# Attention values as wide products in an encoder block: one product of 256 columns instead of two of 128, with the evacuations, tile rings and load queues that go with it

## The chip, the cores and the metric

The kernel runs on one core of a Trainium2 chip. The metric is the device time of one execution in microseconds (us). The kernel before was run three times; a separate execution was profiled.

## The reference

It is one layer of a hybrid encoder on 1024 tokens of width 1024, all in float32:

```python
h = h + 0.5 * swiglu(rms_norm(h, ffn1_norm[i]), ffn1_w_gate[i], ffn1_w_up[i], ffn1_w_down[i])
u = rms_norm(h, mix_norm[i])
z = u @ w_in[i]
q, k, v, s_in, gates = jnp.split(z, splits, axis=-1)
y_attn = neighbourhood_attention(q, k, v, na_rpb[i]) @ w_attn_out[i]      # 8 heads of 64
y_ssm = s5_branch(s_in, ...) @ w_ssm_out[i]
g_attn, g_ssm = jnp.split(jax.nn.sigmoid(gates), N_BRANCH, axis=-1)
h = h + (g_attn * y_attn + g_ssm * y_ssm) @ w_out[i]
h = h + 0.5 * swiglu(rms_norm(h, ffn2_norm[i]), ffn2_w_gate[i], ffn2_w_up[i], ffn2_w_down[i])
h = h + (p[i] @ ple_w_proj[i]) * jax.nn.sigmoid(rms_norm(h, ple_norm[i]) @ ple_w_gate[i])
...
return rms_norm(h, final_norm)
```

Tokens stand on a grid of 16 rows by 64. In `neighbourhood_attention` a token sees a window of 8 rows by 16 columns that is clamped inside the grid; scores get a learned bias per head and relative place, then softmax, then the weighted sum of the values. `s5_branch` runs a diagonal complex state space layer forward and backward over the tokens, in 32 groups of 16 channels with 64 states each, then a gated linear unit.

## The kernel before

Every float32 product with weights is made of three products of a rounded format (fp32r): an operand is split in a high part, cast by ACT, and the rest, subtracted by DVE (`split`), and `mm3` (L182 to L186) multiplies high by high, high by rest and rest by high into one bank of 128x512. TensorE (PE) runs its instructions in the order of the program. The orders of DVE, ACT, POOL (GpSimd) and SP, which issues most loads, come from a scheduler that plans all engines on a time line of its own.

The order of stages is the first feed-forward block, the mixer, the second feed-forward block, the per-layer input and the last norm (`end`, with the last statistics in `fin[2].stat`). The change lies in the mixer and in `end`.

In the mixer two streams are woven on TensorE. The main one makes the projections of u by `mm3`, of which the gate tiles (`gt`) and the q and k tiles come last. The side stream is a generator, `mixer_side`, which gets a turn every few `mm3`. It works through 64 attention units (8 heads, two halves of the rows `rb`, four blocks of columns `cb`). At step j:

- `attn_scores` of unit j: two products of q with the high and the rest of k into `s` (288 or 384 columns); DVE adds the bias and takes the maximum, ACT makes the softmax `sm`.
- `attn_turn` of unit j-3: three transposes of `sm` into bank `pt`; ACT casts `pth` from it, DVE subtracts `ptl`.
- `attn_values` of unit j-5: for each of three groups of keys one product of `pth` with 128 weight columns (`vhl`: 64 of the high part of v and 64 of the rest) and one of `ptl` with the 64 high columns alone, each over 128 query columns of a bank `O`. One bank takes the four `cb` of a half. After the fourth, ACT copies the lower 64 partitions (`ol`), DVE adds (`ot`), and the queue of ACT stores 64x512 to `o_d` in DRAM.
- `scan_steps(2)`: two steps of the state space scan on POOL, three instructions each (L1092 to L1094), 128 steps in all on the states X.
- from j = 48 on: `ssm_out` of a pair of groups, which issues four loads (`emi`: output matrices from `e_d` and inputs from `u_d`, two each, L1102 and L1103) and copies states to `xs`; three steps later `go` of that pair makes its outputs `yo` with two products L1117 and four L1119, which ACT copies to `ys` and stores.

After that come the gated linear unit, the loads of both branches (`load_br`: `br` from `o_d` for b = 0, from `y2_d` for b = 1, through a ring of three tiles of 128x1024 called "st"), the branch products, and the output projection, whose weights `wblk` POOL loads with an accumulating load (L415).

Tiles come from rings: "hid", 56 tiles of 128x512, of which u takes 32; "w", 12 tiles of 128x1024; "tmp", 4; "st", 3. TensorE writes to 8 banks of 128x512.

Of the kernel before, what the change touches and what calls it, by code (L numbers as in the profile page):

```python
# [8 lines left out]
F32 = mybir.dt.float32  # L9
# [7 lines left out]
P = 128  # L17
SEQ = 1024
HT = 512
# [19 lines left out]
def encoder_block(ctx, tc, I, out):  # L39
# [76 lines left out]
    o_d = dtile("o_d", [512, SEQ])  # L116
    g_d = dtile("g_d", [16, P, SEQ])
    y_d = dtile("y_d", [NPD, P, NCH])
    y2_d = dtile("y2_d", [512, SEQ])
# [81 lines left out]

        return tc.issue_after(mark["ins"]) if "ins" in mark else nullcontext()

    def rstd(m, r, q):
        A.activation(r, m, AF.Abs_reciprocal_sqrt, bias=eps)
        V.tensor_tensor(q, r, r, ALU.mult)
        V.scalar_tensor_tensor(q, m, eps, q, ALU.add, ALU.mult)
        V.scalar_tensor_tensor(r, q, -3.0, r, ALU.add, ALU.mult)

    class Norm:  # L210
# [33 lines left out]
        def stat(self, r=None, summed=False):  # L244
            if summed:
                m = self.acc
            else:
                m = bank("ms")[:, 0:self.n]
                sums = [self.acc] + self.more
                for i, sq in enumerate(sums):  # L250
                    T.matmul(m, lhsT=ones, rhs=sq, start=i == 0, stop=i == len(sums) - 1)
            q = tmq("rq", [P, self.n])
            r = thid("rs", [P, self.n], F32) if r is None else r
            rstd(m, r, q)
            self.r = r

        def apply(self, gi, res, every):
# [839 lines left out]
    def ssm_out(pr):  # L1097

        ms = []
        for g in range(2):  # L1100
            em = thid("emi", [P, 4, NCH], F32)
            nc.sync.dma_start(em[:, 0:3].rearrange("p a b -> p (a b)"), e_d[2 * pr + g])  # L1102
            nc.sync.dma_start(em[:, 3], u_d[2 * pr + g])  # L1103
            ms.append(em)

        xs = tw("xs", [P, 2, 2, NCH], F32)
        for g in range(2):
            for r in range(2):
                s0 = Xv[g * 64:(g + 1) * 64, r, pr, 0:1]
                both = bass.AP(tensor=s0.tensor, offset=s0.offset, ap=[list(s0.ap[0]), [NCH + 2, 2], [1, NCH]])  # L1110
                (A.copy if g == r else V.tensor_copy)(xs[r * 64:(r + 1) * 64, g], both)

        def go():
            o = bank("yo")
            for g in range(2):
                oo = o[:, g * NCH:(g + 1) * NCH]
                T.matmul(oo, lhsT=ms[g][:, 0], rhs=ms[g][:, 3], start=True, stop=False)  # L1117
                for d in range(2):
                    T.matmul(oo, lhsT=ms[g][:, 1 + d], rhs=xs[:, g, d], start=False, stop=(d == 1))  # L1119
            ys = tmp("ys", [P, 2, NCH])  # L1120
            A.copy(ys, o[:, 0:2 * NCH].rearrange("p (g c) -> p g c", g=2))
            nc.scalar.dma_start(y_d[2 * pr:2 * pr + 2].rearrange("g p c -> p g c"), ys)
        return go
# [10 lines left out]
    def qk_proj(hp, wq, wk):  # L1134
        qs, kh, kl = [], [], []
        for t in range(2):
            o = proj(wq, t, "q")
            for i in range(2):
                if t == 0:
                    qs.append(tw("qs"))  # L1140
                src = o[i * 64:(i + 1) * 64].rearrange("p (r b c) -> p r b c", r=8, b=4)
                hs, ls = slice(i * 64, (i + 1) * 64), slice((1 - i) * 64, (2 - i) * 64)

                def view(sl):
                    return qs[i][sl, hsl(t)].rearrange("p (b r c) -> p r b c", b=4, r=8)
                A.copy(view(hs), src)
                V.tensor_tensor(view(ls), src, view(hs).bitcast(F32), ALU.subtract)
        for t in range(2):
            o = proj(wk, t, "k")
            for i in range(2):  # L1150
                if t == 0:
                    kh.append(tw("kh"))
                    kl.append(tw("kl"))
                hs, ls = slice(i * 64, (i + 1) * 64), slice((1 - i) * 64, (2 - i) * 64)
                A.activation(kh[i][hs, hsl(t)], o[hs], AF.Copy, scale=0.125)
                A.activation(kh[i][ls, hsl(t)], o[hs], AF.Copy, scale=0.125)
                for s_ in (hs, ls):
                    V.scalar_tensor_tensor(kl[i][s_, hsl(t)], o[hs], 0.125, kh[i][hs, hsl(t)].bitcast(F32),
                                           ALU.mult, ALU.subtract)
        for i in range(2):  # L1160
            qkv[2 * hp + i] = (qs[i], kh[i], kl[i])

    def load_v(hd, cb):
        n = 4 * KNC[cb]
# [33 lines left out]
    def attn_scores(hd, rb, cb):  # L1198
        q, kh, kl = qkv[hd]
        n = KNC[cb]  # L1200
        nk = 12 * n
        qv = q[:, rb * HT + cb * P:rb * HT + (cb + 1) * P]
# [12 lines left out]
        V.reciprocal(st[:, 2:3], st[:, 1:2])  # L1215
        A.activation(sm, sm, AF.Copy, scale=st[:, 2:3])
        return sm

    def attn_turn(cb, sm):
        kp = 4 * KNC[cb]  # L1220
        tp = bank("pt")
        for g in range(3):
            T.transpose(tp[0:kp, ksl(g)], sm[:, g * kp:(g + 1) * kp], ident)
# [4 lines left out]
        return ph, pl  # L1228

    def attn_values(hd, rb, cb, O, ph, pl):  # L1230
        kp = 4 * KNC[cb]
        hl = vld[hd, cb]
        for g in range(3):

            T.matmul(O[:, ksl(cb)], lhsT=hl[0:kp, rb + g].rearrange("p h d -> p (h d)"), rhs=ph[0:kp, ksl(g)], start=(g == 0), stop=False,
                     skip_group_check=True)
            T.matmul(O[0:64, ksl(cb)], lhsT=hl[0:kp, rb + g, 0], rhs=pl[0:kp, ksl(g)], start=False, stop=(g == 2),
                     skip_group_check=True)
        if cb == 3:
            ot, ol = tmp("ot"), tmp("ol")  # L1240
            A.copy(ol[0:64], O[64:128])
            V.tensor_tensor(ot[0:64].rearrange("p (r b c) -> p b r c", r=8, b=4),
                            O[0:64].rearrange("p (b r c) -> p b r c", b=4, r=8),
                            ol[0:64].rearrange("p (b r c) -> p b r c", b=4, r=8), ALU.add)
            nc.scalar.dma_start(o_d[hd * 64:(hd + 1) * 64, hsl(rb)], ot[0:64])


    ydr = y_d.rearrange("g (t o) c -> g o t c", o=16)
# [37 lines left out]
    def mixer_side():  # L1286
# [31 lines left out]
        for j in range(n + 6):  # L1318
            if j < n:
# [3 lines left out]
                if cb == 0 and j > 0:  # L1323
                    make_tabs(hd, rb)
                sms[j] = attn_scores(hd, rb, cb)
            if 0 <= j - 3 < n:
                pts[j - 3] = attn_turn(units[j - 3][2], sms.pop(j - 3))
            if 0 <= j - 5 < n:
                hd, rb, cb = units[j - 5]
                if cb == 0:  # L1330
                    O[hd, rb] = bank("O")
                attn_values(hd, rb, cb, O[hd, rb], *pts.pop(j - 5))
                if rb == 1 and hd + 1 < NH:
                    load_v(hd + 1, cb)
            scan_steps(2)
            if j >= SO:
                p = j - SO
# [62 lines left out]
    def load_br(t, b):  # L1400

        res = []
        if b == 0:
            for k in range(0, 4, 2):
                st = tst("br")
                nc.sync.dma_start(st.rearrange("p (k c) -> p k c", k=2),
                                  o_d[k * P:(k + 2) * P, hsl(t)].rearrange("(k p) c -> p k c", p=P))
                for i in range(2):
                    hi, lo = tx("bh"), tx("bl")
                    split(hi, lo, st[:, hsl(i)])  # L1410
                    res.append((hi, lo))
            return res
        for k in range(4):
# [264 lines left out]
    def end():  # L1678
# [131 lines left out]
```

## Time and profile before

| | |
|---|---|
| median of three runs | 2099.49 us (2098.23 to 2099.73) |
| profiled execution | 2096.29 us, its span 2094.5 us |
| granted TensorE clock, mean | 0.998 |
| TensorE busy | 2074.5 us, 99% of the span |
| DVE, ACT, POOL busy | 1416.1, 999.6 and 399.4 us |
| last scan step on POOL | starts at 1009.9 us |
| yo products | 1029.0 to 1099.5 us |

Rows of the timeline give start, duration, engine, line, operation, output and inputs, shape; "x3" means three alike in a row, and a bracket at the end the idle time before and what ended it. In a table by stage, the numbers are the length, the busy time of the engines with counts, the clock granted (1.00 is full), the share of the DMA engines that was busy and GB/s. In a tile's rows the three numbers are shortest, median and longest in ns, and then the first and last start in us. Matmuls overlap, so the time of one in a stream is the distance to the next start.

### The profile page before, as it was taken

Reading aid. Unit: us, or ns where it says so; the run is one execution under the profiler, and the core shown is the slowest. Engines: PE = TensorE matmul, PEld = TensorE weight load, DVE = VectorE, ACT = ScalarE, POOL = GpSimd, SP = SyncE. Lnnn points to the kernel's source line nnn. Section 1 sums busy time; section 2 is a strip of 40 time slices with the busy share of each in tenths; the row PEclk is TensorE's granted clock in tenths of the full one; section 3 lists DMA queues with packets and bytes.
Section 4 is the critical chain, followed back from the end, with each engine's and each line's share of the span. In section 5 each row is a group of like instructions: output and inputs, shape, how many; then the busy total and the mean of one; then the engine's idle time right before and its main releaser. Section 6 shows DMA issues by size and latency. Waiting matters only on the chain.

```text
span 2094.5 us, 28063 instructions
## 1 busy us (share of the span) xinstructions
PE 2074.5 (99%) x9662; PEld 1705.4 (81%) x9662; DVE 1416.1 (68%) x2420; ACT 999.6 (48%) x1832; POOL 399.4 (19%) x636
## 2 busy tenths in 40 slices
PE   8999999999999999999999999999999999999998
PEld 3788888888888888888898888788888888888886
DVE  7897776667967334677753668995665665786855
ACT  6434333334445333667774635643333334445543
POOL 0037556441000006888200001000000000000000
PEclk9999999999999999999999999999999999999999
DMA  3435444475533551233477745243324238433302
GB/s 134 143 118 154 125 135 120 144 270 169 188 114 111 159 189 64 70 97 98 123 208 260 247 145 117 77 150 121 100 86 135 82 121 297 155 106 94 118 21 81
DMA packets 197744, 285.19 MB, mean 136 GB/s; under 512 B 41569, under 2 KB 81121, under 8 KB 197601
## 3 DMA queue, kind: packets, MB, share of 16 engines
q1 hardware_dynamic: 180304, 258.20, 38.8%
q10 hardware_dynamic: 14992, 21.00, 3.0%
q0 software_dynamic: 2304, 4.20, 1.2%
q8 instruction: 76, 1.25, 0.2%
q14 instruction: 68, 0.55, 0.1%
HBM read 201.01 MB, written 82.31 MB: 135 GB/s over the span
## 4 chain that ended last, share of the span: by engine, by line
PE 94%; DVE 2%; ACT 1%; DMA 1%; SPq 0%; issue 0%; DVEq 0%; ACTq 0%
PE dx L184 4%; PE dx L185 4%; PE dx L186 4%; PE gx L184 3%; PE ux L184 3%; PE ux L186 3%; PE gx L186 3%; PE gx L185 3%; PE ux L185 3%; PE gt L184 3%; PE gt L185 3%; PE gt L186 3%; PE dy L186 2%; PE dy L184 2%; PE dy L185 2%; PE gy L184 2%
## 5 line engine op out<-in xcount | busy, mean ns | idle before, releaser
L153 ACT CAST wh<-hbuf 128x512 fp32r<-128x512 f32 x280 | 173.0, 622 | 392.3 <-PE gx L185 80.9
L154 DVE TENSOR_TENSOR wl<-hbuf,wh 128x512 fp32r<-128x512 f32 x280 | 209.2, 750 | 122.7 <-ACT wh L153 120.5
L153 ACT CAST wh<-wblk 128x512 fp32r<-128x512 f32 x190 | 118.0, 622 | 192.6 <-PE dx L185 83.2
L154 DVE TENSOR_TENSOR wl<-wblk,wh 128x512 fp32r<-128x512 f32 x190 | 130.6, 690 | 49.3 <-ACT wh L153 41.8
L184 PE MATMUL dx<-ah,wh 128*128 128x512 f32 x416 | 163.3, 393 | 0.3 <-DVE hbuf L688 0.3
L186 PE MATMUL dx<-ah,wl 128*128 128x512 f32 x416 | 161.9, 389 | 0.0
L185 PE MATMUL dx<-al,wh 128*128 128x512 f32 x416 | 161.8, 389 | 0.0
L1092 POOL TENSOR_TENSOR sc<-X,rho 128x128 f32<-128x128 f32 x128 | 77.9, 609 | 327.2 <-ACT X L1075 317.3
L154 DVE TENSOR_TENSOR al<-araw,ah 128x512 fp32r<-128x512 f32 x154 | 106.3, 694 | 50.1 <-PE dx L185 21.1
L184 PE MATMUL gx<-xh,wh 128*128 128x512 f32 x320 | 124.9, 390 | 1.2 <-DVE c L575 1.2
L184 PE MATMUL ux<-xh,wh 128*128 128x512 f32 x320 | 125.0, 390 | 0.0
L186 PE MATMUL ux<-xh,wl 128*128 128x512 f32 x320 | 124.5, 389 | 0.0
L185 PE MATMUL gx<-xl,wh 128*128 128x512 f32 x320 | 124.5, 389 | 0.0
L186 PE MATMUL gx<-xh,wl 128*128 128x512 f32 x320 | 124.5, 389 | 0.0
L185 PE MATMUL ux<-xl,wh 128*128 128x512 f32 x320 | 124.5, 389 | 0.0
L153 ACT CAST ah<-araw 128x512 fp32r<-128x512 f32 x154 | 94.9, 619 | 43.2 <-PE dx L185 12.6
L184 PE MATMUL gt<-xh,wh 128*128 128x512 f32 x256 | 102.7, 401 | 0.0
L186 PE MATMUL gt<-xh,wl 128*128 128x512 f32 x256 | 99.8, 390 | 0.0
L185 PE MATMUL gt<-xl,wh 128*128 128x512 f32 x256 | 99.8, 390 | 0.0
L422 DVE TENSOR_TENSOR hbuf<-hbuf 128x512 f32<-128x512 f32 x120 | 91.4, 762 | 2.1
L184 PEld LDWEIGHTS dx<-ah,wh 128*128 128x128 f32 x416 | 78.1, 188 | 17.8 <-issue 0.7
L185 PEld LDWEIGHTS dx<-al,wh 128*128 128x128 f32 x416 | 78.1, 188 | 16.9 <-issue 0.7
(381 smaller groups left out, 5590.2 us busy)
## 6 DMA issues: line engine op xcount, KB each, us to landing
araw<-a_d SPq DMA_DIRECT2D x154, 256.0 KB
a_d<-c SPq DMA_DIRECT2D x148, 256.0 KB
wblk<-in_wd SPq DMA_DIRECT2D x88, 256.0 KB
hbuf<-in_wg SPq DMA_DIRECT2D x40, 512.0 KB
hbuf<-in_wu SPq DMA_DIRECT2D x40, 512.0 KB
wst<-in_win SPq DMA_DIRECT2D x26, 512.0 KB
hbuf<-in_xT SPq DMA_DIRECT2D x32, 256.0 KB
h_d<-hbuf ACTq DMA_DIRECT2D x32, 256.0 KB
```

The lines of the kernel that those rows point to most:

```text
L153: A.copy(hi, src)
L154: return eng.tensor_tensor(lo, src, hi.bitcast(F32), ALU.subtract)
L184: T.matmul(o, lhsT=wh, rhs=xh, start=first, stop=False, skip_group_check=more)
L185: T.matmul(o, lhsT=wh, rhs=xl, start=False, stop=False, skip_group_check=more)
L186: T.matmul(o, lhsT=wl, rhs=xh, start=False, stop=last, skip_group_check=more)
L422: V.tensor_tensor(b11, (b12, b22, None, None, b21)[i - 2], b11, ALU.subtract)
L1092: G.tensor_tensor(sc, both, rho4, ALU.mult)
```

## The change

It has five parts.

1. The transposed probabilities go to one tile `ptb` of 3 groups x (high, rest) x 128 columns from a ring of two, and `attn_values` makes one product of 256 columns per group. The rest is now multiplied by the rest of v too; that quarter of the bank is not used. A bank `O` takes two `cb` instead of four. After each pair ACT copies 128x256 and DVE adds 64x256; both halves of the partitions (products with the high and with the rest of v) are stored as two planes of `o_d`, 32 stores instead of 16. `load_br` for b = 0 loads both planes (8 loads instead of 4), DVE adds them in 128x1024, and the split undoes the order of the blocks.
2. At each step the values now come ahead of the transposes.
3. The q tiles and the states `xs` come from the "hid" ring (q as four tiles of 512 instead of two of 1024 for a pair of heads); the "w" ring has 10 tiles instead of 12.
4. The 64 `emi` loads are issued by GpSimd.
5. In `end`, two scalings on ACT, `scaled(6)` and `scaled(7)`, move behind the reciprocal root of the last statistics.

```diff
-    def rstd(m, r, q):
+    def rstd(m, r, q, mid=None):
         A.activation(r, m, AF.Abs_reciprocal_sqrt, bias=eps)
+        if mid is not None:
+            mid()
...
-    cur.update(st=(ap_, "st", 3), w=(ap_, "w", 12), tmp=(ap_, "tmp", 4))
+    cur.update(st=(ap_, "st", 3), w=(ap_, "w", 10), tmp=(ap_, "tmp", 4))
...
-            nc.sync.dma_start(em[:, 0:3].rearrange("p a b -> p (a b)"), e_d[2 * pr + g])
-            nc.sync.dma_start(em[:, 3], u_d[2 * pr + g])
+            G.dma_start(em[:, 0:3].rearrange("p a b -> p (a b)"), e_d[2 * pr + g])
+            G.dma_start(em[:, 3], u_d[2 * pr + g])
...
-        xs = tw("xs", [P, 2, 2, NCH], F32)
+        xs = thid("xs", [P, 2, 2, NCH], F32)
...
-        ph = thid("pth", [P, 384])
-        pl = thid("ptl", [P, 384])
-        A.copy(ph[0:kp], tp[0:kp, 0:384])
-        V.tensor_tensor(pl[0:kp], tp[0:kp, 0:384], ph[0:kp].bitcast(F32), ALU.subtract)
+        pb = ap_.tile([P, 3, 2, P], F32R, tag="ptb", bufs=2, name="ptb")
+        src = tp[0:kp, 0:384].rearrange("p (g q) -> p g q", g=3)
+        A.copy(pb[0:kp, :, 0], src)
+        V.tensor_tensor(pb[0:kp, :, 1], src, pb[0:kp, :, 0].bitcast(F32), ALU.subtract)
...
+        o = O["o"][:, (cb % 2) * 256:(cb % 2) * 256 + 256]
         for g in range(3):
-            T.matmul(O[:, ksl(cb)], lhsT=hl[0:kp, rb + g].rearrange("p h d -> p (h d)"), rhs=ph[0:kp, ksl(g)], start=(g == 0), stop=False,
+            T.matmul(o, lhsT=hl[0:kp, rb + g].rearrange("p h d -> p (h d)"), rhs=pb[0:kp, g].rearrange("p h q -> p (h q)"), start=(g == 0), stop=(g == 2),
                      skip_group_check=True)
-            T.matmul(O[0:64, ksl(cb)], lhsT=hl[0:kp, rb + g, 0], rhs=pl[0:kp, ksl(g)], start=False, stop=(g == 2),
-                     skip_group_check=True)
-        if cb == 3:
-            ot, ol = tmp("ot"), tmp("ol")
-            A.copy(ol[0:64], O[64:128])
...
-            nc.scalar.dma_start(o_d[hd * 64:(hd + 1) * 64, hsl(rb)], ot[0:64])
+        if cb % 2 == 0:
+            return
+        ot = ap_.tile([P, 256], F32, tag="ot", bufs=2, name="ot")
+        ov = ot.rearrange("p (b q) -> p b q", b=2)
+        src = O["o"].rearrange("p (b h q) -> p h b q", b=2, h=2)
+        A.copy(ov, src[:, 0])
+        V.tensor_tensor(ov[0:64], src[0:64, 1], ov[0:64], ALU.add)
+        nc.scalar.dma_start(o_d[:, hd * 64:(hd + 1) * 64, rb * HT + (cb - 1) * P:rb * HT + (cb + 1) * P], ot)
...
-                st = tst("br")
...
+                st = [tst("br") for _ in range(2)]
+                for w in range(2):
+                    nc.sync.dma_start(st[w].rearrange("p (k c) -> p k c", k=2),
+                                      o_d[w, k * P:(k + 2) * P, hsl(t)].rearrange("(k p) c -> p k c", p=P))
+                V.tensor_tensor(st[0], st[0], st[1], ALU.add)
...
-        scaled(6, six[3])
         added(a, b, s, hm)
         fin[2].square(7, V)
-        scaled(7, hm)
         finish(1, (4, 6))
-        fin[2].stat()
+        fin[2].stat(mid=lambda: (scaled(6, six[3]), scaled(7, hm)))
```

How this stands on the engines: on TensorE, one unit in the middle of the stage before, from its scores to the gate products behind it (line, operation, output<-inputs, shape).

```order
L1207 MATMUL s<-kh,qs 128x384
L1208 MATMUL s<-kl,qs 128x384
L1223 MATMUL pt<-ident,sm 128x128 x3
L1235 MATMUL O<-pth,vhl 128x128
L1237 MATMUL O<-ptl,vhl 64x128
L1235 MATMUL O<-pth,vhl 128x128
L1237 MATMUL O<-ptl,vhl 64x128
L1235 MATMUL O<-pth,vhl 128x128
L1237 MATMUL O<-ptl,vhl 64x128
L184 MATMUL gt<-xh,wh 128x512
L185 MATMUL gt<-xl,wh 128x512
```

Six products on two kinds of weights stand between the transposes and the gate products. The same unit on TensorE after:

```order
L1209 MATMUL s<-kh,qs 128x384
L1210 MATMUL s<-kl,qs 128x384
L1239 MATMUL O<-ptb,vhl 128x256 x3
L1225 MATMUL pt<-ident,sm 128x128 x3
L184 MATMUL gt<-xh,wh 128x512
L185 MATMUL gt<-xl,wh 128x512
L186 MATMUL gt<-xh,wl 128x512
```

Three products stand ahead of the transposes; all other rows of TensorE keep their order. On SP before, a piece of the stage in which the emi loads are issued (`bt` are bias tables, `wst` weights of the projection, `g_d<-gs` stores of gates, `vf` values):

```order
L1181 DMA bt<-in_rpbw 128x384
L161 DMA wst<-in_win 128x1024
L1102 DMA emi<-e_d 128x384
L1103 DMA emi<-u_d 128x128
L1102 DMA emi<-e_d 128x384
L1103 DMA emi<-u_d 128x128
L1364 DMA g_d<-gs 128x512
L1167 DMA vf<-v_d 96x1x64 x4
L1167 DMA vf<-v_d 128x1x64 x2
L1102 DMA emi<-e_d 128x384
L1103 DMA emi<-u_d 128x128
```

The emi loads stood among others on SP. On POOL after, from the last scan step on:

```order
L1094 TENSOR_TENSOR sc<-X,rho 128x128
L1095 TENSOR_TENSOR sc<-sc 128x64
L1096 TENSOR_TENSOR X<-sc,X 128x32x2
L1104 DMA emi<-e_d 128x384
L1105 DMA emi<-u_d 128x128
L1104 DMA emi<-e_d 128x384
L1105 DMA emi<-u_d 128x128
```

All 64 moved behind the last step of the scan on POOL; behind them stand the 16 loads of `wblk`, which before followed the scan directly.

More of the change, by code (lines that the diff above doesn't have):

```diff
@@ L115, in encoder_block @@
     v_d = dtile("v_d", [SEQ, 512])
-    o_d = dtile("o_d", [512, SEQ])
+    o_d = dtile("o_d", [2, 512, SEQ])
     g_d = dtile("g_d", [16, P, SEQ])
@@ L1138, in qk_proj @@
             for i in range(2):
-                if t == 0:
-                    qs.append(tw("qs"))
+                q = thid("qs")
+                qs.append(q)
                 src = o[i * 64:(i + 1) * 64].rearrange("p (r b c) -> p r b c", r=8, b=4)
@@ L1160, in qk_proj @@
         for i in range(2):
[L1161 removed]
+            qkv[2 * hp + i] = (qs[i::2], kh[i], kl[i])
     def load_v(hd, cb):
@@ L1201, in attn_scores @@
         nk = 12 * n
-        qv = q[:, rb * HT + cb * P:rb * HT + (cb + 1) * P]
+        qv = q[rb][:, ksl(cb)]
         def kv(kt):
@@ L1325, in mixer_side @@
                 sms[j] = attn_scores(hd, rb, cb)
+            if 0 <= j - 5 < n:
+                hd, rb, cb = units[j - 5]
+                if cb % 2 == 0:
+                    O.setdefault((hd, rb), {})["o"] = bank("O")
+                attn_values(hd, rb, cb, O[hd, rb], pts.pop(j - 5))
+                if rb == 1 and hd + 1 < NH:
+                    load_v(hd + 1, cb)
             if 0 <= j - 3 < n:
                 pts[j - 3] = attn_turn(units[j - 3][2], sms.pop(j - 3))
[L1328 to L1334, printed above, removed]
             scan_steps(2)
@@ L1404, in load_br @@
             for k in range(0, 4, 2):
-                st = tst("br")
-                nc.sync.dma_start(st.rearrange("p (k c) -> p k c", k=2),
-                                  o_d[k * P:(k + 2) * P, hsl(t)].rearrange("(k p) c -> p k c", p=P))
+                st = [tst("br") for _ in range(2)]
[3 more added lines that the diff above has]
+                V.tensor_tensor(st[0], st[0], st[1], ALU.add)
                 for i in range(2):
                     hi, lo = tx("bh"), tx("bl")
-                    split(hi, lo, st[:, hsl(i)])
+                    sv = st[0][:, hsl(i)].rearrange("p (b r c) -> p r b c", b=4, r=8)
+                    hv, lv = (x.rearrange("p (r b c) -> p r b c", b=4, r=8) for x in (hi, lo))
+                    split(hv, lv, sv)
                     res.append((hi, lo))
```

13 lines of the change are left out of this document (5 added, 8 removed).

## The prediction

> **What bounds the kernel now.** I read the page's busy line and chain first, then a table by stage of the stretch that the change touches (from 840 to 1110 us; the evacuations of the values, quoted in part 4, start between 864.6 and 1107), then TensorE's timeline of single units.
>
> ```profile
> PE 2074.5 (99%) x9662; PEld 1705.4 (81%) x9662; DVE 1416.1 (68%) x2420; ACT 999.6 (48%) x1832; POOL 399.4 (19%) x636
> PE 94%; DVE 2%; ACT 1%; DMA 1%; SPq 0%; issue 0%; DVEq 0%; ACTq 0%
> 840.00:1110.00 270.00, 268.93 (x1655) 236.13 (x1654) 181.21 (x444) 188.18 (x425) 146.36 (x306) 1.00 0.42 122
> ```
>
> TensorE is busy 99% of the span and makes up 94% of the chain. In the touched stretch (third row: length, then busy time of PE, PEld, DVE, ACT and POOL) it is busy 268.93 of 270 us at full clock, while DVE and ACT have about 80 us free each and POOL 124. So what leaves TensorE's stream here shortens the kernel, as long as no other engine starts to hold it up.
>
> **1. Value products (192 of 128 query columns with 128 weight columns, and 192 with 64, become 192 of 256 columns).** The first seven rows below are a unit in the middle of the stage, from its transposes to its fourth gate product; the four after them are a unit that has no values yet, so that its transposes stand right ahead of the gate product; the last two are 256-column products of the end of the kernel.
>
> ```profile
> 909.69 0.49 PE L1223 MATMUL pt<-ident,sm 128*128 128x128 f32 x3
> ...
> 910.08 0.22 PE L1237 MATMUL O<-ptl,vhl 96*64 96x128 f32 x1
> 910.14 0.27 PE L1235 MATMUL O<-pth,vhl 96*128 96x128 f32 x1
> 910.25 0.22 PE L1237 MATMUL O<-ptl,vhl 96*64 96x128 f32 x1
> 910.31 0.28 PE L1235 MATMUL O<-pth,vhl 96*128 96x128 f32 x1
> ...
> 910.48 0.44 PE L184 MATMUL gt<-xh,wh 128*128 128x512 f32 x1
> ...
> 911.23 0.39 PE L184 MATMUL gt<-xh,wh 128*128 128x512 f32 x1
> 844.65 0.49 PE L1223 MATMUL pt<-ident,sm 128*96 128x128 f32 x3
> 844.89 0.48 PE L184 MATMUL gt<-xh,wh 128*128 128x512 f32 x1
> 845.21 0.39 PE L185 MATMUL gt<-xl,wh 128*128 128x512 f32 x1
> ...
> 845.68 0.39 PE L184 MATMUL gt<-xh,wh 128*128 128x512 f32 x1
> 2076.01 0.28 PE L186 MATMUL pg<-xh,whl 128*128 128x256 f32 x1
> 2076.37 0.28 PE L186 MATMUL pg<-xh,whl 128*128 128x256 f32 x1
> ```
>
> Durations overlap on a pipelined TensorE, so I count from start to start. Before, transposes, values and three gate products take 911.23 - 909.69 = 1.54 us. Without values the same transposes and gate products take 845.68 - 844.65 = 1.03 us. Three products of 256 columns take 2076.37 - 2076.01 = 0.36 us, 0.12 each. With the values ahead of the transposes the unit becomes 1.03 + 0.36 = 1.39 us and saves 0.15. The difference comes from this: a product with 128 weight columns costs 910.25 - 910.14 = 0.11 and the one with 64 behind it 0.06, together 0.17 for a pair; one wide product costs 0.12 and does the work of both.
>
> How many units: values are computed at steps 5 to 68 of the loop; from step 51 to 66 the state space outputs follow in the same step. So 46 plain units give 46 x 0.15 = 6.9 us. The two last have no transposes: 3 x 0.17 - 0.36 = 0.15 each, 0.3 together. In the other 16 the transposes now stand ahead of the yo products:
>
> ```profile
> 1028.18 0.49 PE L1223 MATMUL pt<-ident,sm 128*96 128x128 f32 x3
> ...
> 1028.98 0.44 PE L1117 MATMUL yo<-emi 128*128 128x128 f32 x2
> 1029.25 0.61 PE L1119 MATMUL yo<-xs,emi 128*128 128x128 f32 x4
> 1029.70 0.39 PE L1117 MATMUL yo<-emi 128*128 128x128 f32 x2
> 1029.92 0.61 PE L1119 MATMUL yo<-xs,emi 128*128 128x128 f32 x4
> ```
>
> From the transposes to the second yo group is 1029.25 - 1028.18 = 1.07 us. After: 0.36 for the values, 844.89 - 844.65 = 0.24 for the transposes, 1029.92 - 1029.70 = 0.22 for two yo products, and about 0.09 that the first product behind transposes took over the others (845.21 - 844.89 = 0.32 against (845.68 - 845.21) / 2 = 0.23). That is 0.91, so 16 x 0.16 = 2.6 us. Sum for TensorE: 6.9 + 2.6 + 0.3 = 9.8 us. Bounds: if the extra 0.09 also falls on the new place of the values behind the scores in all 64 units, 64 x 0.09 = 5.8 is lost and 4 stays; if a 256-column product behind its like takes half of a 512-column one (0.23 / 2 = 0.115), 192 x 0.005 = 1 more is gained. I take the unit rows as they are.
>
> [...]
>
> **2. Waits that TensorE has now.** Two touch this stretch (duration waited in brackets; in the second row total, times, longest):
>
> ```profile
> 1038.92 0.49 PE L1117 MATMUL yo<-emi 128*128 128x128 f32 x2 [0.66 <-DVE ot L1242]
> PE yo L1117 <- DMA emi<-u_d: 0.4, 1, 0.4
> ```
>
> The first waits for a bank that the 512-column evacuation held; the second for a late emi load on SP. With O evacuated by halves and emi on an empty queue, part of these 1.1 us may go; I count 0.7 gained. New small waits I put at 0.5. Together nothing to speak of: + 0.2.
>
> **3. The 64 emi loads move from SP to GpSimd.** On GpSimd they stand behind the last scan step and ahead of 16 accumulating loads.
>
> ```profile
> L1102 SPq DMA_DIRECT2D emi<-e_d x32: 319/382/911, 1017.3 to 1088.3; - x32
> L1117 PE MATMUL yo<-emi x64: 275/275/377, 1029.0 to 1099.0; 128*128 128x128 f32 x64
> 1009.87 0.39 POOL L1094 TENSOR_TENSOR X<-sc,X 128x64 f32<-128x64 f32 x1
> L415 POOL DMA_DIRECT2D wblk<-in_wout x16: 853/865/1170, 1238.5 to 1280.4; - x16
> DMA to landing us min/median/max: 4.1/7.0/8.3
> L415 POOL DMA_DIRECT2D wblk<-in_wout x16 | 14.1, 932 | 256.9 <-ACT wblk L414 256.7 <-issue 0.2
> L1092 POOL TENSOR_TENSOR sc<-X,rho x128: 495/528/1774, 798.3 to 1008.9; 128x128 f32<-128x128 f32 x128
> ```
>
> The scan ends at 1010.3 and runs without TensorE, so it does not come earlier. Four loads serve one step; on GpSimd the only issue in the trace is the wblk load, 0.853 to 1.170 us, mean 0.932. First step: 1010.3 + 4 x 0.93 + 7.0 (median landing) = 1021.0; TensorE wants it at 1029.0 - 46 x 0.15 = 1022. It fits by 1 us. Last step: 1010.3 + 64 x 0.932 + 7.0 = 1077; TensorE wants it at about 1098.2 - 9.4 = 1088.8. The limit for one issue is (1088.8 - 7.0 - 1010.3) / 64 = 1.12 us. The fastest wblk issue, slowed as GpSimd's own 128x128 operation is slowed (609 mean in the wide stage against 495 at best, 1.23), gives 1.05, still below; the worst row, 1.17, is above it by 64 x 0.05 = 3.4 us. From below: emi loads that cost GpSimd only what SP pays (0.38) gain nothing, since TensorE is not behind them. I take 0.93, the mean of the nearest row, and no cost. The wblk loads start at 1238.5, far behind. SP loses 64 rows at about 0.4 us; what is queued behind them there (gate stores, loads of br and of weights) can only come earlier.
>
> **4. Smaller pieces.**
>
> ```profile
> L1241 ACT COPY ol<-O x16: 582/583/587, 864.6 to 1107.0; 64x512 f32<-64x512 f32 x16
> L1242 DVE TENSOR_TENSOR ot<-O,ol x16: 671/683/683, 865.2 to 1107.6; 64x512 f32<-64x512 f32 x16
> L1245 ACTq DMA_DIRECT2D o_d<-ot x16: 452/453/507, 865.9 to 1108.3; - x16
> L1121 ACT COPY ys<-yo x16: 352/372/374, 1031.0 to 1100.7; 128x256 f32<-128x256 f32 x16
> L1406 SPq DMA_DIRECT2D br<-o_d x4: 370/370/451, 1116.4 to 1144.5; - x4
> L184 PE MATMUL br<-bh,wh x32: 389/389/389, 1168.0 to 1189.1; 128*128 128x512 f32 x32
> ```
>
> Evacuation: ACT pays 32 x 0.372 instead of 16 x 0.583, + 2.6 us, and 16 more store issues at 0.453, + 7.2; DVE 32 additions of 256 columns instead of 16 of 512, each no dearer than the 0.683 that it replaces, so at most + 10.9. All in 250 us in which each has about 80 us free: nothing on the path. Branch inputs: 8 loads instead of 4, and 4 DVE additions of 128x1024, by an estimate 1.4 us each (twice the 0.683 of 512 columns). The last load now starts at 1144.5 and the products that need it at 1168; four more loads through three slots, a few us each, eat into 23 us of slack without using it up. Smaller tiles for q and states and the w ring of 10 instead of 12 change who waits for a slot: by the trace nothing there waits on it, cost zero, bounded by the 1.07 us that separates the busy time from the stretch's length.
>
> Tail:
>
> ```profile
> 2084.57 0.89 ACT L1655 ACTIVATE hbuf<-hbuf,gains 128x256 f32<-128x256 f32 x2
> 2084.60 0.70 PE L251 MATMUL ms<-sq,ones 128*128 128x256 f32 x2 [0.70 <-DVE sq L232]
> 2085.37 0.45 ACT L205 ACTIVATE rs<-ms,eps 128x256 f32<-128x256 f32 x1
> 2087.29 0.69 DVE L1671 TENSOR_TENSOR hbuf<-hbuf,rs 128x512 f32<-128x512 f32 x1
> ```
>
> The two scalings end at 2085.46 and the root starts at 2085.37, 0.07 after its sums end at 2085.30. Moved behind the root they run under DVE's chain, until 2087.29. Gain 0 to 0.1, taken as 0.
>
> **Sum.** 9.8 + 0.2 = 10 us off a span of 2094.5, so 2084.5. The profiled execution took 2096.29 us, 3.2 under the median of 2099.49; I subtract the 10 from the median: 2089.5. Its own range is 7 to 13 us gained.
>
> **Rivals.**
> - Larger gain (over 13 us): both waits go and wide products cost 0.115: 9.8 + 1 + 1.1 = 11.9; over 13 needs one more piece. 2086 or less, chance 0.04.
> - Gain handed back: the first yo step waits for scan end plus loads (a landing of 8.3 and four issues of 1.17 make 1023.3, 1.3 late), or the branch loads run late, or the values behind the scores pay 0.09 each (5.8). Time 2093 to 2099, chance 0.14, half of it within 0.2%.
> - Columns set the price: 384 x 128 columns equal 192 x 256. Then 2099, chance 0.04. Against it stands the pair of 0.17 us where the 64-column-weight product takes 0.06 and the other 0.11.
> - Slower: GpSimd's issue becomes the bound of the last 16 steps. It decides where one issue costs over 1.12 us, takes the whole gain at about 1.27 ((9.8 / 64) more), and passes 0.2% at 1.34. At 1.4 the last loads land (1.4 - 1.12) x 64 = 18 us late: 2107. For it: GpSimd's 128x128 operation goes from 495 to 1774 ns while DVE is busy. Against it: 1.17 is the worst of 16. Chance 0.08 with lesser mishaps. [...]
>
> **How the numbers follow.** Forecast 0.70, larger 0.04, handed back 0.14, columns 0.04, slower 0.08. 0.2% is 4.2 us, about what a measurement of this kernel can tell from no change. Faster: 0.70 + 0.04 + half of 0.14 = 0.81. Same: 0.07 + 0.04 = 0.11. Slower 0.08. The range, 2085 to 2097, takes in the forecast, half of the larger gain and two thirds of what is handed back, and leaves out 0.02 + 0.05 + 0.04 + 0.08 = 0.19.
>
> **What the profile after will show if this is right.** 192 O products of 128x256 about 0.12 us apart; a plain unit of 1.39 us between its values and the fourth gate product; 64 DMA issues of about 0.9 us on POOL from 1010 on; no wait of yo over 1 us; a stage up to 840 and from 1170 of the same length as before. Wrong would be: wide products at 0.15 or more, POOL rows over 1.12 us with TensorE waiting for emi, or branch products that wait for DVE.

## The result, and the profile after

The changed kernel takes 2117.01 us (median of four runs, 2116.26 to 2120.02) against 2099.09 before: 1.0089 of the time, 95% interval 1.0077 to 1.0101. It is slower by 18 us, where 10 us less were forecast. Its profiled execution took 2120.02 us (span 2118.2, mean clock 0.993), so the two profiled executions differ by 23.7 us. The busy line and the shares of the chain on the page after:

```profile
PE 2078.7 (98%) x9470; PEld 1704.5 (80%) x9470; DVE 1421.8 (67%) x2440; ACT 998.7 (47%) x1850; POOL 435.2 (21%) x700
PE 44%; DVE 2%; DMA 2%; ACT 1%; issue 0%; SPq 0%; ACTq 0%; DVEq 0%
```

Less work on TensorE would have shown as fewer busy us. The instructions did fall from 9662 to 9470, but the busy time did not. The shares of the chain sum to 49%: it could be followed back over about half of the span only, so they don't compare with the 94% before; but transfers now stand in it with 2% of the whole span. The table by stage tells why (the columns are those of the table before; the last row is a short stretch behind one stall, told below):

```profile
840.00:1110.00 270.00, 254.98 (x1379) 220.85 (x1378) 177.46 (x452) 180.68 (x429) 182.98 (x376) 0.97 0.41 122
1050.00:1110.00 60.00, 49.13 (x284) 43.80 (x283) 25.79 (x76) 37.19 (x88) 16.90 (x32) 0.89 0.59 168
1110.00:1160.00 50.00, 44.52 (x205) 36.83 (x204) 15.69 (x23) 20.28 (x34) 0.00 (x0) 0.93 0.70 217
1073.00:1079.00 6.00, 5.53 (x22) 4.97 (x23) 3.43 (x12) 5.12 (x15) 1.07 (x2) 0.62 0.36 76
```

Before, TensorE was busy 268.93 of the same 270 us at full clock. Now it idles for 15 us of them and runs at a clock of 0.97. Nearly all of this falls in the late steps, when the emi loads and the state space outputs have joined: up to 1010 us TensorE idles for 0.7 us at full clock, from 1050 to 1110 for 10.9 us at a clock of 0.89 (second row). The branch products, the first work behind the stage, start late; before, it was at 1168.0 us:

```profile
L184 PE MATMUL br<-bh,wh x32: 389/389/389, 1192.8 to 1213.9; 128*128 128x512 f32 x32
```

That is 24.8 us, and the rest of the kernel takes 1.1 us less than before. The first scores start at 837.0 us against 835.2, so 1.8 us of it lie ahead of them; the other 23 lie between the first scores and the branch products. These are the waits of TensorE there (line that waits, what ended it, total us, times, longest):

```profile
PE yo L1119 <- DVE stat L1213: 8.0, 2, 5.2
PE O L1239 <- DVE ptb L1229: 7.6, 6, 4.6
PE pt L1225 <- ACT gs L1368: 2.8, 1, 2.8
PE s L1210 <- DVE kl L1160: 1.1, 1, 1.1
PE s L1209 <- DVE ot L1249: 0.9, 1, 0.9
```

Together 20.4 us, against 1.1 before. By an estimate from the rows above, a granted clock of 0.97 over 270 us and 0.93 over 50 us costs about 8 + 3.5 = 11.5 more. So some 31 us were lost where this part grew by 23; the 8 or so between them are of the size of the saving that was forecast.

The products themselves became as cheap as forecast. A unit in the middle of the stage, from TensorE's timeline:

```profile
902.10 0.52 PE L1239 MATMUL O<-ptb,vhl 128*128 128x256 f32 x3
902.45 0.49 PE L1225 MATMUL pt<-ident,sm 128*96 128x128 f32 x3
902.70 0.48 PE L184 MATMUL gt<-xh,wh 128*128 128x512 f32 x1
903.01 0.39 PE L185 MATMUL gt<-xl,wh 128*128 128x512 f32 x1
903.25 0.39 PE L186 MATMUL gt<-xh,wl 128*128 128x512 f32 x1
903.48 0.40 PE L184 MATMUL gt<-xh,wh 128*128 128x512 f32 x1
```

The unit takes 903.48 - 902.10 = 1.38 us (forecast 1.39), three wide products 902.45 - 902.10 = 0.35. Of the 14 plain units of this kind between 860 and 1005 us, 12 take 1.38 or 1.39; before, all 14 take 1.53 or 1.54.

The waits name DVE and ACT, but both have some 90 us free. Much of what they wait for is a transfer. Waits of ACT from 840 to 1170 us for the loads of the values, before:

```profile
ACT vhl L1170 <- DMA vf<-v_d: 4.2, 6, 1.8
```

and after:

```profile
ACT vhl L1172 <- DMA vf<-v_d: 35.0, 12, 7.3
```

The loads are the same 128 transfers of the same tensor. One stall shows how a late load reaches TensorE. First rows of SP's timeline in the kernel after (a row's x3 means three issues), then two transfers from its chain of waits (start, duration until landed, what):

```profile
1060.62 2.48 SPq L1169 DMA_DIRECT2D vf<-v_d  x3
1065.11 0.62 SPq L1169 DMA_DIRECT2D vf<-v_d  x1
...
1068.88 2.81 SPq L1169 DMA_DIRECT2D vf<-v_d  x4
1061.02 7.43 DMA y_d<-ys
...
1070.66 5.35 DMA vf<-v_d
```

The first four issues load one tile of values. By their last semaphore updates they land 8.0, 7.5, 6.8 and 7.0 us after their issue, the last at 1072.06; it had been held until a `yt` load of 1059.74, which had its semaphore, landed at 1065.09. A store of `o_d` had gone out at 1059.16 and landed at 1065.29. That it made the transfers beside it late is not shown by this stall; the experiments on the layout test it. The store of outputs at 1061.02 holds a `yt` load on SP and with it the next four loads of values; the last of those lands at 1076.01, and the next cast starts at 1076.11. Now ACT and TensorE in the timeline:

```profile
1072.08 0.40 ACT L1172 CAST vhl<-vf 96x256 fp32r<-96x256 f32 x1 [7.30 <-DMA vf<-v_d]
1067.79 0.49 PE L1225 MATMUL pt<-ident,sm 128*96 128x128 f32 x3
1073.47 0.79 PE L1119 MATMUL yo<-emi 128*128 128x128 f32 x2 [5.19 <-DVE stat L1213]
1076.62 0.63 PE L185 MATMUL gt<-xl,wh 128*128 128x512 f32 x1
1077.05 0.61 PE L186 MATMUL gt<-xh,wl 128*128 128x512 f32 x1
```

ACT stood 7.30 us at the cast of the first of these tiles, and what comes behind it in ACT's order waited too; TensorE stood 5.19 us. Its next gate products are 0.43 us apart instead of 0.23, at the clock of 0.62 in the last row of the table by stage. The 4.63 us stall that ends at 1126.5 looks alike: a clock of 0.56 from 1126 to 1133. So these two stalls are paid twice: as idle time and as slow products behind them.

Landing times, worked out from the last semaphore update of each transfer between 840 and 1010 us, median and longest: the store of `o_d` went from 2.7 (2.9) us to 5.7 (8.6), the load of `vf` from 2.6 (3.9) to 3.5 (7.8). The store moves 128 KB in both kernels. The share of the DMA engines that is busy (tenths of 16, in 40 slices of the window) shows the difference. From 876.2 to 879.2 us in the kernel after, with the row of ACT's queue:

```profile
DMA  9974589767731111101110111111111101111111
q10 hardware_dynamic: 113, 0.12, 10.9%
```

and over the same length, 867.2 to 870.2, before:

```profile
DMA  1176949493523221110000000000000000000001
q10 hardware_dynamic: 80, 0.13, 17.4%
```

Before, a store passes as a burst on most engines and is gone in half the window. After, a tenth of the engines stays busy to the end: two streams, which take one packet of 1 KB each about every 0.042 us. The new destination is `o_d[:, 64 rows, 256]`, and its outermost dimension has 2 entries, one per plane. Each such store has 3 updates of its completion semaphore, one 0.93 us (median) after its issue and two towards its end, and 2 packets of 4 B beside its 128 of 1 KB; each store of the kernel before has 16 updates and 16 such packets beside 64 of 2 KB. No engine is named in these records: that the new store runs on two of them is an estimate from the two streams and these counts.

### The profile page after: what moved, and what is told of

Same layout as the page of the kernel before. It is cut to its first block, busy times and chain, and to the rows that moved or that the text cites. A ratio compares the mean times of both kernels' runs of the same rounds, so it can differ in the third digit from the quotient of the medians.

```text
span 2118.2 us, 27817 instructions
## 1 busy us (share of the span) xinstructions
PE 2078.7 (98%) x9470; PEld 1704.5 (80%) x9470; DVE 1421.8 (67%) x2440; ACT 998.7 (47%) x1850; POOL 435.2 (21%) x700
```

## Experiments

The theories, by the letters that the expectations use. **A**: with the emi rows gone from SP, the `yt` loads, which wait for stores of `y_d`, stand ahead of `vf` loads. **B**: the emi loads on GpSimd are themselves late or in the way. **C**, with **F**: the wide products, or ACT's and DVE's new work around them, starve TensorE. **D**: twice as many stores on ACT's queue make more waits through the completion semaphores that all transfers of SP and ACT share in turn. **E**: the smaller rings. **H**, formed after the first eight runs: the store in two planes runs on two DMA engines, lands late, and delays what shares them. Each ratio is to the kernel before on the same chip.

**Emi loads back on SP, and part 4 alone.** Both are two lines:

```diff
-            G.dma_start(em[:, 0:3].rearrange("p a b -> p (a b)"), e_d[2 * pr + g])
-            G.dma_start(em[:, 3], u_d[2 * pr + g])
+            nc.sync.dma_start(em[:, 0:3].rearrange("p a b -> p (a b)"), e_d[2 * pr + g])
+            nc.sync.dma_start(em[:, 3], u_d[2 * pr + g])
```

> The changed kernel with its part 4 undone: the 64 emi loads go out from SP again; wide values, order, rings and tail stay. Theory A (the order on SP): without the emi rows SP's list lets the yt loads, which wait for stores of y_d, in front of vf loads that attention needs; with emi back, SP's list has all but one yt load behind the last vf load, so the stalls go: 2088 to 2093 us. Theory B (GpSimd issues or lands emi too late): the same, 2088 to 2093. Theory C (wide values, with the rings and evacuations by halves, starve TensorE by themselves): about 2117, no better than the changed kernel.

> The kernel before with part 4 alone: emi loads issued by GpSimd, everything else as before. In its list on SP, 8 of the 32 yt loads stand in front of the last 8 vf loads (in the changed kernel 17 yt rows stand among the last vf loads, spread over 5 places). Theory A: slower than before, 2101 to 2112, with ACT waiting for vf as in the changed kernel but fewer times. Theory B: slower by what the changed kernel lost, 2115 or more. Theory C: 2097 to 2100, no change.

With the loads back on SP nothing was won: 2117.89 us, 1.0092 (1.0077 to 1.0107). So neither A nor B explains the loss by itself. On the kernel before, the same two lines the other way cost 9 us: 2107.52, 1.0045 (1.0028 to 1.0061). The parts don't add up. With the loads on SP the waits of SP name the store:

```profile
SPq L1169 <- DMA o_d<-ot: 14.9, 10, 3.5
SPq L1105 <- DMA o_d<-ot: 12.2, 3, 4.7
SPq L1260 <- DMA o_d<-ot: 5.0, 3, 1.8
PE yo L1119 <- DMA emi<-u_d: 10.2, 7, 3.5
```

Three kinds of loads that have nothing to do with `o_d` wait for its store to land, and TensorE now waits for late emi loads (last row). The traces have one reason for it: the transfers of SP and ACT, 1226 in the kernel before and 1182 after, take turns on eight completion semaphores (147 to 154 on each; the next one on it comes 8 later in the median). None of them is issued before the one that had its semaphore last has landed; the `vf` load of 1065.11 went out 0.02 us after that. That fits D, and it fits any slow store.

**The order on SP (A).** In one kernel the `yt` loads also go to GpSimd; in the other they stay on SP, but come only behind the last `vf` load that has been issued:

```diff
-    nc.sync.dma_start(yv[g*16:(g+1)*16], ydr[8*m+g])
+    with tc.issue_after(vld["last"].ins): nc.sync.dma_start(yv[g*16:(g+1)*16], ydr[8*m+g])
```

> The changed kernel, and the 32 yt loads too are issued by GpSimd, between its emi loads. SP's list then holds nothing between gate stores, bias tables and vf loads. Theory A: the waits of ACT for vf go, 2088 to 2096; some yo may wait, as a yt load that waits on GpSimd now holds up emi. Theory B: GpSimd has 32 issues more, so 2117 or slower. Theory C: about 2117.

> The changed kernel with one rule of order more: the yt loads stay on SP, but none may be issued ahead of the last vf load. emi stays on GpSimd. Theory A: the waits of ACT for vf (22.9 us in the changed kernel) all but go, 2090 to 2098. Theory B and theory C: about 2117, since neither GpSimd's issues nor the values change.

On GpSimd it got worse, 2122.82 us, 1.0116 (1.0100 to 1.0131): the wait only moved, ahead of emi loads (waits of POOL, 960 to 1150 us).

```profile
POOL yt L1260 <- DMA y_d<-ys: 44.4, 7, 17.4
```

Behind `vf` it is 2113.95, 1.0072 (1.0057 to 1.0087), 3 us less than the change with overlapping intervals. A is at most a small part.

**Number of stores (D), one larger store, wide products alone (C).** `two_stores` is the kernel before with each store cut in two halves of 64x256. `one_store` and `one_store_sp` are the change with one store of both planes, 2x64x512, for four column blocks, emi on GpSimd or on SP. `wide_lean` is the kernel before with wide products alone, summed before one store of 64x512 as it was.

```diff
+            for w in range(2): nc.scalar.dma_start(o_d[hd*64:(hd+1)*64, rb*HT+w*256:rb*HT+w*256+256], ot[0:64, w*256:w*256+256])
...
+        if cb == 3: nc.scalar.dma_start(o_d[:, hd*64:(hd+1)*64, hsl(rb)], O["t"])
```

> The kernel before with each of the 16 stores of o_d split in two halves of 256 columns: 32 stores on ACT, as in the changed kernel, and nothing else. Theory D: in the compiled programs all loads and stores that SP and ACT issue share eight completion semaphores in turn, so that a load on SP waits until the transfer eight places ahead of it has landed; a store on ACT lands late (SP waited 12.2 us for o_d ahead of emi and 11.2 ahead of vf with emi back on SP), and twice the stores means twice the waits. By D: 2102 to 2112. Theory E (the smaller rings: q tiles and states among the 56 tiles, 10 weight tiles) and theory F (the work of ACT and DVE at the head changes of the late stage): 2097 to 2101.

> The changed kernel with emi on SP, and one store of o_d per four column blocks (two planes of 64x512) instead of two: 16 stores as before. The evacuations stay by two blocks, into one tile of 512 from the tmp ring, which gets the freed space as a fifth tile. Theory D: SP's waits for o_d about halve, 2095 to 2107 against 2118. Theories E and F: 2113 to 2120.

> The same with emi on GpSimd, so the changed kernel with 16 stores instead of 32. Theory D alone: 2098 to 2108 against 2117. D and A together (yt ahead of vf on SP still costs what part 4 alone cost, about 9 us): 2104 to 2112. Theories E and F: 2112 to 2119.

> The kernel before with the 192 products of 256 columns and nothing else of the change: the high and rest parts lie side by side in two tiles of the 56, banks take two column blocks, ACT and DVE add them into one tile of 512, and one store of 64x512 goes out as before; order, rings, emi and branch loads as before. It has two more small operations of ACT and of DVE per unit. If the TensorE saving of 0.165 us a unit is real and the losses come from the other parts (D or E), 2088 to 2094. If the values by wide products starve TensorE by themselves (F), 2100 or more.

Twice the stores cost nothing: 2098.14 us, 1.0001 (0.9991 to 1.0010). D as a matter of number falls. Half the stores in larger pieces of two planes made it worse: 2135.11, 1.0183 (1.0167 to 1.0198) with emi on SP and 2126.14, 1.0141 (1.0124 to 1.0159) on GpSimd. Their stores take 9.2 us to land. This result led to H: not how many stores, but how one is laid out. `wide_lean` lost too, 2110.10, 1.0058 (1.0043 to 1.0073), and by another wait:

```profile
PE O L1235 <- DVE ptb L1227: 10.2, 9, 3.2
```

It also casts and subtracts `ptb` in two pieces and keeps the transposes ahead of the values. Which of these makes `ptb` late was not separated, so it says nothing of the product alone.

**Layout of the store (H).** The change with each store of two planes issued as two of one plane, with emi on GpSimd, on SP, and with `yt` behind `vf`; and the kernel before with a second, useless store of the same tile into a scratch tensor of two planes.

```diff
-        nc.scalar.dma_start(o_d[:, hd*64:(hd+1)*64, ...], ot)
+        for w in range(2): nc.scalar.dma_start(o_d[w, hd*64:(hd+1)*64, ...], ot[w*64:(w+1)*64])
...
+            nc.scalar.dma_start(scr[:, hd*32:(hd+1)*32, hsl(rb)], ot[0:64])
```

> The changed kernel with one edit: each store of o_d (two planes of 64x256 in one transfer) goes out as two transfers of one plane each, 64 instead of 32. Theory H: by the trace's semaphore events the store of two planes lands 4.8 to 8.6 us after its issue (median 5.7 between 840 and 1010 us; 9.2 where one store took 512 columns), the kernel before's 64x512 store 2.7, its halves 2.4; its packets run one behind the other in two streams, so it uses two of the 16 DMA engines and everything that crosses these two waits (vf up to 7.8 us against 3.9). By H the landings return to 2 to 4 us and the waits of ACT for vf, of SP for o_d and y_d fall; the order of yt on SP (theory A, +9 us by the run with emi alone) stays: 2096 to 2106, against 2117. Theory F (ACT and DVE at the head changes) and the number of stores: 2115 to 2121.

> The same with emi back on SP, so without part 4: H and A both gone. H: 2088 to 2096, faster than before by most of the 9.8 us that the values save. If something else in parts 1 to 3 costs (F, rings, the eight branch loads): 2100 or more.

> Stores by planes, emi on GpSimd, and no yt load ahead of the last vf load on SP: H and A mended without undoing part 4. H with A: 2088 to 2098. If GpSimd's issues themselves cost: 2100 or more.

> The kernel before with a second store behind each of its 16 stores of o_d, of the same tile, into a scratch tensor of two planes (2x32x512) that nothing reads; the output is the reference's. The run with each store cut in two by columns (32 stores) cost nothing. H: this store lands in 4 to 6 us on two engines and delays the transfers beside it: 2101 to 2112. If stores of two planes are harmless: 2096 to 2100.

Cutting the store in two took the time from 2117 to 2096.94 us, 0.9994 (0.9985 to 1.0004): 20 us for one edited line that moves the same bytes with twice the issues. Stores land in 2.3 us (longest 4.8) and `vf` loads in 2.5. The stage, and ACT's waits for `vf`:

```profile
840.00:1110.00 270.00, 261.96 (x1462) 228.70 (x1461) 179.39 (x457) 186.75 (x439) 181.67 (x376) 0.99 0.47 137
ACT vhl L1172 <- DMA vf<-v_d: 13.2, 5, 5.0
```

TensorE's busy time rose from 254.98 to 261.96 us and its clock from 0.97 to 0.99; ACT waits 13.2 us instead of 35.0. The other way round, 16 useless stores of two planes cost the kernel before 11 us, 2110.16, 1.0055 (1.0042 to 1.0067), while 16 additional plain stores (`two_stores`) cost nothing. The loads on SP then wait for the scratch tensor:

```profile
SPq L1167 <- DMA scr<-ot: 15.7, 6, 3.6
SPq L1102 <- DMA scr<-ot: 3.4, 1, 3.4
```

H holds in both directions. The second has a gap: the useless stores also move 128 KB more each, which `two_stores` does not, and the same bytes in a plain layout were not run; the first has none, since its bytes are the same. With the store mended, emi on SP gives 2094.18, 0.9976 (0.9968 to 0.9985), and `yt` behind `vf` with emi on GpSimd 2094.81, 0.9978 (0.9969 to 0.9987): 2.8 and 2.1 us less than with emi on GpSimd and `yt` ahead.

**The price of the layout by itself.** This program only stores a tile, three times in each shape, one transfer after the other.

> No part of the block is computed: on an idle core ACT's queue stores one tile, three times in each of eight shapes, each store waiting for the one before to land; then zeros go out. Shapes: 64x256, 128x256, 2x64x256, 4x32x256, 8x16x256, 16x8x256 (the leading number counts planes apart in DRAM), 2x64x512 and 64x512. Theory H, one DMA engine per plane: from issue to landing 2 us for 64x256, 128x256 and 16x8x256, about 2.7 more for 2x64x256 (64 packets of 42 ns one behind the other on each of two engines), about 1.3 more for 4x32x256, 0.6 for 8x16x256; for 2x64x512 about 5 more. If the number of bytes or rows sets it: all shapes of 128 rows alike.

The second of each three, from the chain (start, duration until landed):

```profile
5.08 1.91 DMA half<-t
13.07 1.80 DMA full<-t
23.69 4.75 DMA two<-t
38.64 3.22 DMA four<-t
49.96 2.59 DMA eight<-t
59.68 2.30 DMA sixteen<-t
74.23 7.72 DMA twolong<-t
94.16 2.25 DMA halflong<-t
```

`half` is 64x256 (64 KB). `full` is 128x256; `two`, `four`, `eight` and `sixteen` are the same 128 KB in that many planes. 4.75 us falls to 2.30 as the outermost dimension grows from 2 to 16. `twolong` is 2x64x512, 256 KB, and takes 5.5 us more than its half of 64x512. Against `full`, two planes cost 2.95 us more, four 1.42 and eight 0.79, where H expected 2.7, 1.3 and 0.6. The order of these rows fits H, one engine per plane, and so does the number of semaphore updates in the trace: 3, 5 and 9 for the stores of two, four and eight planes, 16 for all others. In the kernels each `vf` load has 5, like `four`: its source is 4 rows of the grid by columns by 64 values. So by an estimate from these counts the loads that suffer most are themselves on four engines; whether that is why they suffer was not run.

**One dimension of 128, part 4 once more, and the best version.** `rows128_sp` stores 128x256 in one transfer into `o_d` as [8, 128, tokens], which takes 16 loads for the branch. `emi_yt_behind` is part 4 alone on the kernel before, with `yt` behind `vf`. `one_plane_sp` and `one_plane` keep the wide products and both halves, but ACT copies the upper half and DVE adds twice, so that one plane of 64x256 is stored and the branch has its four loads as before; emi on SP or on GpSimd.

```diff
+        nc.scalar.dma_start(o_d[hd, :, rb*HT+(cb-1)*P:rb*HT+(cb+1)*P], ot)
...
-        A.copy(ov, src[:, 0])
-        V.tensor_tensor(ov[0:64], src[0:64, 1], ov[0:64], ALU.add)
-        nc.scalar.dma_start(o_d[:, hd*64:(hd+1)*64, ...], ot)
+        A.copy(ov[0:64], src[64:128, 0])
+        for h in range(2): V.tensor_tensor(ov[0:64], src[0:64, h], ov[0:64], ALU.add)
+        nc.scalar.dma_start(o_d[hd*64:(hd+1)*64, ...], ot[0:64])
```

> Parts 1 to 3 and 5 of the change with emi on SP, and o_d laid out as 8 heads x 128 rows, so that one transfer of 128 rows x 256 columns stores both planes (32 stores, not 64); the branch loads become 16 of 64 partitions. Theory H (a transfer spreads over the DMA engines by its outermost dimension): the store lands in 2 to 3 us as the single planes do, and the time is that of the run with stores by planes, 2091 to 2097. If it was the bytes or the 32 stores of 128 rows: 2110 or more.

> The kernel before with part 4 alone (2107.5 in its run) and no yt load ahead of the last vf load on SP. Theory A (the order on SP costs): 2097 to 2101, no change against before. Theory B (emi from GpSimd costs by its issues, its landing or by what it displaces): 2104 to 2110.

> Wide values, rings and tail as in the change, emi on SP; DVE now adds all three parts (ACT copies the lower 64 partitions, DVE adds twice), so that one plane of 64x256 is stored, 32 times, and the branch loads are the four of the kernel before. Both the store in two planes and the additional branch loads (2.8 + 0.9 us of waits and a slow clock behind them at the first branch product of the run with rows of 128) are gone. If the remaining loss was in these: 2088 to 2093, the full 10 us. If the late steps starve by their own (F): 2094 to 2100.

> The same with emi issued by GpSimd, as in the change: what part 4 costs where the store is no longer slow. By the two runs with stores by planes (2096.9 and 2094.2) 2 to 4 us over the run before this one; by emi alone on the kernel before, 9.

`rows128_sp` took 2096.30, 0.9990 (0.9981 to 0.9999). Its stores land in 1.8 us, but its branch products now wait for their 16 loads, 3.0 us in all:

```profile
PE br L184 <- ACT bh L153: 2.6, 1, 2.6
PE br L185 <- DVE bl L154: 0.4, 1, 0.4
```

`emi_yt_behind` is at 2105.81, 1.0039 (1.0026 to 1.0053), so A is not what part 4 costs alone. `one_plane_sp` is the fastest, 2091.63, 0.9964 (0.9951 to 0.9977), ahead of both kernels by 7 and 25 us; `one_plane` takes 2109.34, 1.0042 (1.0031 to 1.0054). ACT's waits for `vf` in the one with emi on SP:

```profile
ACT vhl L1172 <- DMA vf<-v_d: 3.9, 5, 1.3
```

and with emi on GpSimd:

```profile
ACT vhl L1172 <- DMA vf<-v_d: 18.9, 11, 5.3
```

Between 1015 and 1105 us, while the emi loads run, the `vf` loads land in 2.8 us (median) with emi on SP and in 4.5 with emi on GpSimd. Part 4 thus cost 17.7 us here by the medians (2 to 4 or 9 were expected), 9 on the kernel before, 2.8 with plane stores and about nothing (-0.9) beside the slow stores. The profiles of this pair show less than the medians: `one_plane_sp` was profiled in its slowest execution, 2096.00, and `one_plane` in its fastest, 2104.10. That the values come late in these runs is seen; why loads from GpSimd delay them, and so unevenly, stays open.

## Why the prediction was wrong

**Part 1 (value products)** held: 1.38 us a unit against 1.39. `one_plane_sp`, which keeps part 1 and has neither the slow stores nor part 4, gains 6.95 us; its interval, 4.8 to 10.3 us, includes the forecast 10. In its late steps TensorE waits 1.4 + 1.0 + 0.9 + 0.7 = 4.0 us, but in the profiled execution, which at 2096.00 us was 4 us slower than the other four; where the median lost what is missing of the 10 is not shown.

**Part 2 (waits)** put new small waits at 0.5 us. They came to 20.4, against 1.1 before.

**Part 4 of the prediction (smaller pieces)** is the step that failed, in the sentence on the evacuation: "16 more store issues at 0.453 ... nothing on the path". The store was priced by its issue row, and its time to land was not asked for. The issue row hardly moved, 0.453 to 0.502 us (medians); the landing went from 2.7 to 5.7 us. I also took what a transfer delays to be only what reads its data: nothing reads `o_d` before the branch, but loads on SP wait for its semaphore. Undoing this alone gives back 20 of the 28 us between forecast and result. How much of the 20 goes by the DMA engines that transfers share, and how much by the semaphores that they share, no run separates. Of the other 8, part 4 of the change takes 2.8 once the stores are quick; the rest is open.

**Part 3 of the prediction (emi on GpSimd)** was safe on the price and wrong on the rest. One issue costs 0.535 us (medians of 0.536 from `e_d` and 0.534 from `u_d`), below the 0.93 taken from another kind of load and far below the 1.12 at which TensorE would wait for it:

```profile
L1104 POOL DMA_DIRECT2D emi<-e_d x32: 536/536/765, 1013.4 to 1091.4; - x32
L1119 PE MATMUL yo<-emi x64: 274/275/580, 1027.3 to 1116.6; 128*128 128x128 f32 x64
```

The first output came at 1027.3, 5 us later than forecast, when its four emi loads had landed by 1021.7: the time was lost ahead of it, 1.8 us of it before the first scores. The price did not set the pace either: 64 issues of 0.535 us are 34 us, but they took 79, since GpSimd waited in between for instructions of TensorE and ACT, up to 6.2 us at a time. The forecast had them follow each other. The rival that ended slower, GpSimd's issue as the bound, did not happen. But "what is queued behind them there ... can only come earlier" failed: the rows that came earlier were `yt` loads that wait for a store, with the `vf` loads behind them.

```profile
SPq L1260 <- DMA y_d<-ys: 30.6, 10, 4.9
```

Moving them back is worth 1.7, 2.1 and 3.1 us by the medians, with emi on GpSimd, in three pairs of kernels whose intervals overlap. The cost of part 4 of the change where stores are quick, 2.8 to 17.7 us, is no term of my sum, and no run explains it.

**The tail** went as forecast: the root starts 0.04 us after its sums, 0.07 before. In TensorE's list of waits neither the smaller rings nor the eight branch loads appear; no run has the rings alone, and with emi on SP the branch products did wait 4.0 + 0.7 us for their inputs. Of the rivals, "columns set the price" is refuted by the 0.35 us for three products, and "gain handed back" named neither the place nor anything near 28 us.

## What to carry to other kernels

A store that nothing reads for a long time can still be on the path (20 us here): look at the dimension that comes first in its access pattern, and at its time to land, not at its issue row or its bytes. Where an output has two planes, store each plane by itself (2117.01 to 2096.94 us here), or put a long dimension first (2117.89 to 2096.30 with emi on SP). When rows leave a queue, look at what moves up in it and whether that waits for something (here the `yt` loads, 30.6 us on SP).

## What the runs showed of the hardware

- 128 KB (a tile of 128x256) stored as 2 planes of 64x256 lands in 4.75 us, as 128 rows of one plane in 1.80. In the kernel other transfers suffer: `vf` loads, unchanged, go from 2.6 to 3.5 us in the median and from 3.9 to 7.8 at worst.
- The DMA share hides it: 0.42 of the engines were busy in the stage before and 0.41 after, with 122 GB/s in both.
- After a stall of 5.2 us TensorE ran at a clock of 0.62 over 6 us, after one of 4.6 us at 0.56 over 7, its 512-column products 0.43 us apart instead of 0.23.
- A plain load of 192 KB costs GpSimd 0.536 us to issue, against 0.865 for its accumulating loads.
